# Scan outputs of a hybrid encoder layer: four chunks in one step for five of eight groups, with shared probability slots, a part of the decay subtraction on ScalarE and shorter warm-ups

## The chip, the cores and the metric

The kernel runs on one core of one Trainium2 chip. The metric is the device time of one execution in microseconds (us); lower is better. Three runs of the kernel before took 1091.04, 1091.76 and 1092.42 us, so the median is 1091.76 us.

## What is computed

One layer of a bidirectional encoder over 512 tokens of width 1024, in float32. After an RMSNorm, one input projection feeds two branches: a bidirectional chunked state-space scan (8 groups of 4 heads, chunks of 128 tokens) and a windowed attention (16 heads, 64 wide). Gates merge the branches, an output projection and a squared-ReLU MLP follow. The part that matters here is the output of the scan for one direction, for each chunk `l`, group `g` and head `r`:

```python
cb = jnp.einsum('bclgn,bcsgn->bcgls', c, b)
y_diag = jnp.einsum('bcgls,bcgrls,bcsgrp->bclgrp', cb, decay, xdt)
states = jnp.einsum('bclgn,bcgrl,bclgrp->bcgrpn', b, decay_states, xdt)
y_off = jnp.einsum('bclgn,bcgrpn,bcgrl->bclgrp', c, prev, jnp.exp(a_cs))
y = y_diag + y_off        # y_fwd + y_bwd + xs * d_skip, times silu(z), RMSNorm per group
```

In the attention, `p = exp(logits - m)` is divided by its sum before it is multiplied by the values.

## The kernel before, in words

**TensorE's work.** A matrix product in high precision is made of three products of `fp32r` operands: every weight and activation is split into a rounded part and the rest (`hi`, `lo`), and `mm3` issues hi·hi, hi·lo, lo·hi. A projection of 128 output columns over 512 tokens is 24 such matmuls into one PSUM bank of the pool `pp` (3 banks). Everything smaller goes to the pool `ps` (5 banks): transposes, attention scores, the scan's products. The scan's products and transposes are plain `f32`, and a plain `f32` matmul shows as two passes in the trace (a transpose as one).

**Half-width matmuls.** Two kinds of `ps` products write only 64 of 128 partitions, two heads side by side: `m,x` (the scan's diagonal part, `yd`, in `outs`) and `pT,V` (attention values, `attn_values`). In rows they read `128*64`. A stretch of such matmuls that follow each other is called a half-width run below. The other product of `outs` is `C,pv` (the states' part, `yo`, full width, one bank for each chunk).

**Weights.** Each weight chunk is loaded by SyncE's queue (`wr`), rounded by ScalarE (`wh<-wr`, L495) and the rest is made by GpSimd, at times VectorE (`wl<-wr,wh`, L499), three chunks ahead.

**The scan of a group** (`ssd_steps`): `load(c)` fetches rows of cumulative decays, broadcast to 128 partitions (`rf`, `rb`, and `E`); `prep(c)` (L1101 to L1126) makes the 128x128 weights `m` of four heads: GpSimd subtracts the columns `cs` from `rb` for all four heads at once (L1114), ScalarE adds `ncs` to `rf`, head by head (L1116), VectorE takes the minimum of the two (L1117), ScalarE the exponential, and so on; `outs(j)` (from L1128) makes the outputs of the chunks 1 and 0 (`j` = 0) or 2 and 3 (`j` = 1): 6 `C,pv` matmuls, 8 `m,x`, then VectorE's products with `E` (L1151) and the sum `w` (L1152), GpSimd's sums, ScalarE's square `sq` (L1162), GpSimd's `ssq` (L1164) and the split of `ssq` into `sh`, `sl` (L437, L438), which `rms` multiplies by ones on TensorE.

**The attention of a head**: `attn_scores` writes four probability tiles `P` (256, 384, 384 and 256 wide, each in a slot of its own), takes exponentials on ScalarE (L884) and multiplies by the reciprocal sums on VectorE (L890); `attn_flip` transposes them into `pT`; `attn_values` multiplies by `V`.

**The start**: `WARM` matmuls on a tile of zeros, the transpose of `g` (L610 copies it to `gT`), the load of `x`, its scale by ScalarE and VectorE (L640, L641), `DUMMY` matmuls on `x` of which the order puts one ahead of the eight transposes of `x` and the rest behind; VectorE and ScalarE then make `h` (L445, L446).

**What sets the order.** `Quantum`s of projection work give a program order, and `at` places the small steps between them (`SCAN`: `outs` at 2.5 and 5.5). Then a `Planner` with a cost for each instruction re-orders all of it, engine by engine, and `chain` fixes each engine's order. TensorE takes the first ready matmul in program order, but stays with a kind (`fp32r` or `f32`, full or half width) where it can (`next_matmul`), and takes a half-width matmul only when all that its bank waits for is done (`awaited`). Each engine runs its list strictly in that order, so a matmul whose input is late holds all that stand behind it.

Of the kernel before, what the change touches and what calls it, by code (L numbers as in the profile page):

```python
# [11 lines left out]
F32R = mybir.dt.float32r  # L12
AF = mybir.ActivationFunctionType
# [20 lines left out]
BACK = 3  # L34
WARM = 18
DUMMY = 6
COLD = 7000.0
# [41 lines left out]
class Slots:  # L79
# [13 lines left out]
    def put(self, *tiles):  # L93
        for t in tiles:
            self.free.append(self.slot.pop(id(t))[0])


class Planner:
# [13 lines left out]
    def __init__(self, instructions, tags):  # L112
        names = {"PE": "PE", "DVE": "DVE", "Activation": "ACT", "Pool": "POOL", "SP": "SP"}
        self.ins = [i for i in instructions if type(i).__name__ != "BassTilePoolBoundary"]
        self.eng = [names[str(i.engine).split(".")[-1]] for i in self.ins]
        self.tags = tags
        self.depend()
        self.cost = [self.duration(n) for n in range(len(self.ins))]
        self.kind = [self.matmul_kind(n) if e == "PE" else None for n, e in enumerate(self.eng)]
        self.awaited, banks = {}, {}  # L120
        for n, k in enumerate(self.kind):
            if k and k[1]:
                banks.setdefault(self.operands(self.ins[n].outs)[0].tensor.name, []).append(n)
        for bank in banks.values():
            needed = set().union(*(self.pre[n] for n in bank)) - set(bank)
            self.awaited.update((n, needed) for n in bank)

# [234 lines left out]
class Trunk:  # L362
# [498 lines left out]
    def attn_scores(self, h):  # L861
# [3 lines left out]
        mx, sm, es = (self.tmp(n, [128, 4], 4) for n in ("mx", "sm", "es"))  # L865
        P = []
        for n in range(4):
            j0, j1 = (128 if n == 0 else 0), (256 if n == 3 else 384)
            k0, w = n * 128 - 128 + j0, j1 - j0
            ps = self.bank("ps")  # L870
            tok = slice(n * 128, (n + 1) * 128)
            self.mm(ps[:, :w], q[:, tok], self.KH[j][:, k0:k0 + w], True, False)
            self.mm(ps[:, :w], q[:, tok], self.KL[j][:, k0:k0 + w], False, True)
            p = self.slots.get("P", (128, 384))
            nc.vector.tensor_tensor_reduce(p[:, :w], ps[:, :w], bt[:, j0:j1], 1.0, self.sink[:, h:h + 1],
                                           ALU.add, ALU.max, mx[:, n:n + 1])
            P.append((p, w))
# [10 lines left out]
        for n in range(4):  # L888
            p, w = P[n]
            nc.vector.tensor_scalar(p[:, :w], p[:, :w], sm[:, n:n + 1], None, op0=ALU.mult)  # L890
        self.P[h] = P

    def attn_flip(self, h):
        self.T[h] = []
        for n, (p, w) in enumerate(self.P.pop(h)):
# [3 lines left out]
            self.slots.put(p)  # L899
            pT = self.slots.get("pT", (128, 384))  # L900
            (self.nc.vector.tensor_copy if n % 2 else self.nc.scalar.copy)(pT[:, :w], pt[:, :w])
            self.T[h].append((pT, w))

    def attn_values(self, k):
# [12 lines left out]
        for pT, _ in T[0] + T[1]:  # L917
            self.slots.put(pT)
        hi, lo = self.slots.get("ah", dtype=F32R), self.slots.get("al", dtype=F32R)
# [112 lines left out]
    def ssd_steps(self, g):  # L1032
# [71 lines left out]
        def prep(c):  # L1104
            def run():
# [7 lines left out]
                m, n = get("m"), get("n")  # L1113
                nc.gpsimd.tensor_tensor(v4(rb), v4(rb), cs[:, 1].unsqueeze(2).to_broadcast([128, 4, 128]), op=ALU.subtract)  # L1114
                for h in range(4):
# [11 lines left out]

        def outs(j):  # L1128

            def run():  # L1130
                cs = (1, 0) if j == 0 else (2, 3)
                w = st["w"][j]
                yos = {}
                for c in cs:
                    yo = yos[c] = self.bank("ps").rearrange("p (d i t) -> p d i t", d=2, i=2)
                    for d in dirs[3 - c]:
                        for i in range(2):
                            S = st["enter"][c][:, d * 256 + i * 128:d * 256 + (i + 1) * 128]
                            self.mm(yo[:, d, i], S, st["C"][:, c * 128:(c + 1) * 128], True, True)
                yd = self.bank("ps").rearrange("p (c i t) -> p c i t", c=2, i=2)  # L1140
                for c in cs:
                    x, m = xs(c), ch[c]["m"]
                    for i in range(2):
                        for u in range(2):
                            h = 2 * i + u
                            self.mm(yd[u * 64:(u + 1) * 64, c % 2, i], x[:, h * 64:(h + 1) * 64], v4(m)[:, h], True, True)
                    put(m)
                for c in cs:
                    dd = slice(dirs[3 - c][0], dirs[3 - c][-1] + 1)
                    E = ch[c]["E"]  # L1150
                    nc.vector.tensor_tensor(E[:, dd], yos[c][:, dd], E[:, dd], op=ALU.mult)  # L1151
                nc.vector.tensor_tensor(w, yd, w, op=ALU.add)  # L1152
                for c in cs:
                    wc, E = w[:, c % 2], ch[c]["E"]
                    for d in dirs[3 - c]:
                        nc.gpsimd.tensor_tensor(wc, wc, E[:, d], op=ALU.add)  # L1156
                    nc.gpsimd.tensor_tensor(wc, wc, st["z"][j][:, c % 2], op=ALU.mult)
                    put(E)
                if "ssq" not in st:
                    st["ssq"] = get("ssq")  # L1160
                sq = get("sq", (128, 2, 2, 128))
                nc.scalar.activation(sq, w, AF.Square)  # L1162
                half = st["ssq"][:, j * 256:(j + 1) * 256].rearrange("p (c t) -> p c t", c=2)
                nc.gpsimd.tensor_tensor(half, sq[:, :, 0], sq[:, :, 1], op=ALU.add)  # L1164
                put(sq)
                if j == 1:
                    put(st["B"], st["C"], *st["bt"], *st["x"], *st["z"], *st["pv"])
                    hi, lo = st["sq"] = get("sh", dtype=F32R), get("sl", dtype=F32R)
                    self.split(hi, lo, st["ssq"])
                    put(st["ssq"])  # L1170
            return run

        def rms():
# [28 lines left out]

        return weigh, states0, states1, [load(c) for c in range(4)], [prep(c) for c in range(4)], [outs(j) for j in range(2)], rms, finish

# [9 lines left out]
    def place_ssd(self, g, q):  # L1214

        def place():
# [461 lines left out]
```

## Time and profile before

| | before |
|---|---|
| median of 3 runs | 1091.76 us (1091.04 to 1092.42) |
| the profiled execution's own time | 1091.93 us |
| its span, first to last instruction | 1090.1 us |
| TensorE (PE) busy | 1080.1 us (99%) |
| VectorE (DVE) busy | 740.1 us (68%) |
| ScalarE (ACT) busy | 642.9 us (59%) |
| GpSimd (POOL) busy | 794.5 us (73%) |
| mean granted TensorE clock | 0.997 of full speed |

The span lies 1.83 us under the execution's own time, which also holds what lies around the instructions. The profiled execution is 0.17 us above the median. "Busy" counts instructions from start to end as the profile models them; an engine can be busy all the time and still be held up between two of its instructions, so the distances between starts in the timeline are read beside it.

### The profile page before, as it was taken

Reading aid. Unit: us, or ns where it says so; the run is one execution under the profiler, and the core shown is the slowest. Engines: PE = TensorE matmul, PEld = TensorE weight load, DVE = VectorE, ACT = ScalarE, POOL = GpSimd, SP = SyncE. Lnnn points to the kernel's source line nnn. Section 1 sums busy time; section 2 is a strip of 40 time slices with the busy share of each in tenths; the row PEclk is TensorE's granted clock in tenths of the full one; section 3 lists DMA queues with packets and bytes.
Section 4 is the critical chain, followed back from the end, with each engine's and each line's share of the span. In section 5 each row is a group of like instructions: output and inputs, shape, how many; then the busy total and the mean of one; then the engine's idle time right before and its main releaser. Section 6 shows DMA issues by size and latency. Waiting matters only on the chain.

```text
span 1090.1 us, 16770 instructions
## 1 busy us (share of the span) xinstructions
PE 1080.1 (99%) x5631; PEld 906.1 (83%) x5631; DVE 740.1 (68%) x1288; ACT 642.9 (59%) x1379; POOL 794.5 (73%) x977
## 2 busy tenths in 40 slices
PE   9999999999999999999999999999999999999997
PEld 8888888888888888888888888889888888888885
DVE  5567788687788687778788753334672583583698
ACT  6566777686776777676769633323554544544552
POOL 3546657557668888988999876521588898898994
PEclk9999999999999999999999999999999999999998
DMA  7434433634354536354655554534322422424222
GB/s 205 127 95 129 117 94 95 157 90 118 100 123 127 145 101 174 97 141 134 162 138 140 145 173 121 165 103 155 92 70 71 153 74 83 154 74 147 90 97 77
DMA packets 209209, 132.31 MB, mean 121 GB/s; under 512 B 10538, under 2 KB 192042, under 8 KB 209123
## 3 DMA queue, kind: packets, MB, share of 16 engines
q1 hardware_dynamic: 208963, 131.18, 42.6%
q8 instruction: 44, 0.72, 0.3%
q14 instruction: 42, 0.34, 0.1%
q10 hardware_dynamic: 160, 0.07, 0.0%
HBM read 126.69 MB, written 4.52 MB: 120 GB/s over the span
## 4 chain that ended last, share of the span: by engine, by line
PE 98%; DVE 0%; DMA 0%; ACT 0%; issue 0%; POOL 0%; DVEq 0%; POOLq 0%; SPq 0%
PE pp L420 69%; PE ps L420 25%; PE ps L424 3%; DMA rb<-csT 0%; DVEq L1674 0%; DVE ag L1586 0%; DVE h L446 0%; POOLq L1674 0%; ACT h L445 0%; ACT wh L495 0%; SPq L1101 0%; PE pp L424 0%; POOL ssq L1164 0%; ACT x L640 0%; DVE acc L1564 0%
## 5 line engine op out<-in xcount | busy, mean ns | idle before, releaser
L499 POOL TENSOR_TENSOR wl<-wr,wh 128x256 fp32r<-128x256 f32 (+1 forms) x504 | 426.0, 873 | 153.5 <-ACT wh L495 141.7
L420 PE MATMUL pp<-h,wh 128*128 128x512 f32 (+1 forms) x1728 | 527.9, 388 | 0.0
L420 PEld LDWEIGHTS pp<-h,wh 128*128 128x128 f32 x1728 | 318.9, 188 | 64.1 <-issue 1.9
L420 PE MATMUL pp<-h,wl 128*128 128x512 f32 (+1 forms) x856 | 332.3, 388 | 0.0
L495 ACT CAST wh<-wr 128x1024 fp32r<-128x1024 f32 (+1 forms) x133 | 138.9, 1044 | 144.6 <-PE pp L420 125.2
L420 PEld LDWEIGHTS pp<-h,wl 128*128 128x128 f32 x856 | 160.9, 188 | 32.5 <-issue 0.5
L1512 POOL TENSOR_TENSOR wl<-wd,wh 128x256 fp32r<-128x256 f32 x158 | 131.1, 865 | 11.7 <-ACT wh L1509 11.6
L1509 ACT CAST wh<-wd 128x512 fp32r<-128x512 f32 x82 | 47.5, 621 | 32.8 <-PE ps L420 15.5
L420 PE MATMUL ps<-wl,fh 128*128 128x512 f32 x164 | 63.9, 390 | 0.0
L420 PE MATMUL ps<-wh,fl 128*128 128x512 f32 x164 | 63.8, 389 | 0.0
L420 PE MATMUL ps<-wh,fh 128*128 128x512 f32 x164 | 63.8, 389 | 0.0
L1379 DVE SCALAR_TENSOR_TENSOR pp<-pp,r 128x512 f32<-128x512 f32 (+1 forms) x31 | 17.6, 567 | 66.3 <-ACT r L1376 66.3
L1120 ACT ACTIVATE n<-cb,tables 128x128 f32<-128x128 f32 x128 | 49.5, 394 | 17.1 <-DVE cb L1111 16.6
L952 DVE SCALAR_TENSOR_TENSOR u<-pp,cv,u 128x510 f32<-128x510 f32 (+1 forms) x64 | 47.7, 745 | 4.5 <-ACT u L948 3.4
L420 PE MATMUL pp<-yh,wl 128*128 128x512 f32 x128 | 49.8, 390 | 0.0
L420 PE MATMUL pp<-yh,wh 128*128 128x512 f32 x128 | 49.7, 389 | 0.0
L420 PE MATMUL pp<-yl,wh 128*128 128x512 f32 x128 | 49.6, 389 | 0.0
L1121 ACT ACTIVATE m<-cb,tables 128x128 f32<-128x128 f32 x128 | 49.3, 393 | 0.3 <-DVE cb L1111 0.2
L1116 ACT ACTIVATE rf<-rf,tables 128x128 f32<-128x128 f32 x128 | 42.7, 396 | 11.2 <-DMA rf<-csT 11.1
L1156 POOL TENSOR_TENSOR w<-w,E 128x256 f32<-128x256 f32 x48 | 37.9, 803 | 13.1 <-DVE w L1152 11.8
L1050 POOL TENSOR_TENSOR xd<-x,tables 128x256 f32<-128x256 f32 x48 | 33.0, 705 | 17.8 <-ACT x L975 12.8
L884 ACT ACTIVATE P<-P,mx 128x384 f32<-128x384 f32 (+1 forms) x64 | 35.3, 554 | 15.6 <-DVE mx L881 15.3
(271 smaller groups left out, 2163.1 us busy)
## 6 DMA issues: line engine op xcount, KB each, us to landing
wr<-in_w_in SPq DMA_DIRECT2D x76, 512.0 KB, 4.0
wr<-in_w_mlp_in SPq DMA_DIRECT2D x32, 512.0 KB, 4.2
wd<-in_w_mlp_out SPq DMA_DIRECT2D x64, 256.0 KB, 6.3
rf<-csT SPq DMA_DIRECT2D x32, 256.0 KB, 4.8
rb<-csT SPq DMA_DIRECT2D x32, 256.0 KB, 3.7
wr<-in_w_ssd_out SPq DMA_DIRECT2D x14, 512.0 KB, 3.9
E<-csE SPq DMA_DIRECT2D x96, 64.0 KB, 4.2
x<-in_x SPq DMA_DIRECT2D x16, 256.0 KB, 4.2
```

Source lines behind the costliest of these rows:

```text
L420: self.nc.tensor.matmul(out, lhsT, rhs, start=start, stop=stop, skip_group_check=more)
L495: self.nc.scalar.copy(hi[:, :m], raw)
L499: engines[e].tensor_tensor(lo[:, c], raw[:, c], hi[:, c].bitcast(F32), op=ALU.subtract)
L884: nc.scalar.activation(p[:, :w], p[:, :w], AF.Exp, bias=mx[:, n:n + 1], accum_out=sm[:, n:n + 1])
L952: nc.vector.scalar_tensor_tensor(u[:, a:e], ps[:, a + d:e + d], self.wtap(t, b), u[:, a:e], op0=ALU.mult, op1=ALU.add)
L1050: nc.gpsimd.tensor_tensor(v4(xd[:, d * 256:(d + 1) * 256]), v4(xs(c)), by_dir(self.coef, c)[:, d].unsqueeze(2).to_broadcast([128, 4, 64]), ...
L1116: nc.scalar.activation(v4(rf)[:, h], v4(rf)[:, h], AF.Identity, bias=ncs[:, 0, h:h + 1])
L1120: nc.scalar.activation(v4(n)[:, h], cb[:, 0], AF.Copy, scale=dt[:, 0, h:h + 1])
L1121: nc.scalar.activation(v4(m)[:, h], cb[:, 1], AF.Copy, scale=dt[:, 1, h:h + 1])
L1156: nc.gpsimd.tensor_tensor(wc, wc, E[:, d], op=ALU.add)
L1509: nc.scalar.copy(hi, src)
L1512: (nc.vector if q == 512 else nc.gpsimd).tensor_tensor(lo[:, c], src[:, c], hi[:, c].bitcast(F32), op=ALU.subtract)
```

## The change

1. `outs` takes several `j`. For groups 0 to 4 (`JOINT`) one step at 5.5 (`BOTH`) makes all four chunks: the `C,pv` matmuls and `E` products of both halves, then the `m,x` matmuls of both halves (two `yd` banks), then the sums (`collect`). Groups 5 to 7 keep two steps at 2.5 and 5.5.
2. The planner's `awaited` set is made for a whole half-width run of the program order in place of one bank: no matmul of the run is taken before all inputs of the run are done.
3. `rb`: GpSimd subtracts for two of four heads; ScalarE does the other two.
4. The narrow tiles 0 and 3 of `P` and of `pT` share one slot; ScalarE scales these two in place of VectorE.
5. `WARM` goes from 18 to 14, `DUMMY` from 6 to 4.

```diff
+JOINT, BOTH = 5, 5.5
-WARM = 18
-DUMMY = 6
+WARM = 14
+DUMMY = 4
...
-        self.awaited, banks = {}, {}
+        self.awaited, runs, before = {}, [], None
         for n, k in enumerate(self.kind):
             if k and k[1]:
-                banks.setdefault(self.operands(self.ins[n].outs)[0].tensor.name, []).append(n)
-        for bank in banks.values():
-            needed = set().union(*(self.pre[n] for n in bank)) - set(bank)
-            self.awaited.update((n, needed) for n in bank)
+                if not before or not before[1]:
+                    runs.append([])
+                runs[-1].append(n)
+            before = k or before
+        for run in runs:
+            needed = set().union(*(self.pre[n] for n in run)) - set(run)
+            self.awaited.update((n, needed) for n in run)
...
-        P = []
+        P, edge = [], self.slots.get("P")
...
-            p = self.slots.get("P", (128, 384))
+            p = self.slots.get("P", (128, 384)) if 0 < n < 3 else edge[:, n // 3 * 256:n // 3 * 256 + 256]
...
-            nc.vector.tensor_scalar(p[:, :w], p[:, :w], sm[:, n:n + 1], None, op0=ALU.mult)
+            if 0 < n < 3:
+                nc.vector.tensor_scalar(p[:, :w], p[:, :w], sm[:, n:n + 1], None, op0=ALU.mult)
+            else:
+                nc.scalar.activation(p[:, :w], p[:, :w], AF.Copy, scale=sm[:, n:n + 1])
...
-                nc.gpsimd.tensor_tensor(v4(rb), v4(rb), cs[:, 1].unsqueeze(2).to_broadcast([128, 4, 128]), op=ALU.subtract)
+                nc.gpsimd.tensor_tensor(v4(rb)[:, 2:], v4(rb)[:, 2:], cs[:, 1, 2:].unsqueeze(2).to_broadcast([128, 2, 128]), op=ALU.subtract)
+                for h in range(2):
+                    nc.scalar.activation(v4(rb)[:, h], v4(rb)[:, h], AF.Identity, bias=ncs[:, 1, h:h + 1])
...
-        def outs(j):
+        def outs(*js):
             def run():
+                for j in js:
+                    yos = {}
+                    for c in ((1, 0), (2, 3))[j]:
...
+                        yos[c] = yo
+                    for c, yo in yos.items():
+                        dd = slice(dirs[3 - c][0], dirs[3 - c][-1] + 1)
+                        E = ch[c]["E"]
+                        nc.vector.tensor_tensor(E[:, dd], yo[:, dd], E[:, dd], op=ALU.mult)
+                for j in js:
+                    yd = st["yd", j] = self.bank("ps").rearrange("p (c i t) -> p c i t", c=2, i=2)
...
+                for j in js:
+                    collect(j)
...
-            for j in range(2):
-                self.at(q(o["outs"][j]), outs[j])
+            if g < JOINT:
+                self.at(q(BOTH), outs(0, 1))
+            else:
+                for j in range(2):
+                    self.at(q(o["outs"][j]), outs(j))
```

What the planner makes of it, at the two places that the prediction speaks of. TensorE, group 3, in the kernel before: the two half-width runs of the group stand apart, the first among projections (`pp`), the next one some 70 rows further on. Of the first:

```order
L420 MATMUL pp_4457<-h_108,wl_4263 128x512
L420 MATMUL ps_4478<-m_4299,x_3974 64x128 x4
L420 MATMUL ps_4478<-m_4401,x_3974 64x128 x4
L420 MATMUL ps_4529<-C_4082,B_3916 128x128
L420 MATMUL ps_4607<-C_4082,B_3916 128x128
```

And TensorE at the same group in the changed kernel, where the four chunks' `C,pv` and `m,x` stand together:

```order
L425 MATMUL ps_4658<-C_4069,pv_4268 128x128 x4
L425 MATMUL ps_4663<-C_4069,pv_4270 128x128 x2
L425 MATMUL ps_4668<-C_4069,pv_4269 128x128 x4
L425 MATMUL ps_4673<-C_4069,pv_4270 128x128 x2
L425 MATMUL ps_4678<-m_4285,x_3932 64x128 x4
L425 MATMUL ps_4678<-m_4389,x_3932 64x128 x4
L425 MATMUL ps_4687<-m_4494,x_3942 64x128 x4
L425 MATMUL ps_4687<-m_4574,x_3942 64x128 x4
L425 MATMUL pp_4645<-h_98,wh_4483 128x512
```

One half-width run of 16 matmuls (two banks) has taken the place of two of 8, right behind four `C,pv` banks. The same happens once in each of the groups 0 to 4; counted over the whole order, half-width runs go from 24 to 19.

VectorE at the start, before:

```order
L636 ISA junk_125,ssq_75<-x_121 128x512
L636 ISA ssq_75 128x1
L641 TENSOR_SCALAR x_121<-x_121,rst_76 128x512
L610 COPY gT<-ps_80 128x8
L499 TENSOR_TENSOR wl_167<-wr_162,wh_166 128x256 x2
```

And VectorE at the start of the changed kernel:

```order
L641 ISA junk_121,ssq_75<-x_117 128x512
L641 ISA ssq_75 128x1
L615 COPY gT<-ps_80 128x8
L646 TENSOR_SCALAR x_117<-x_117,rst_76 128x512
L504 TENSOR_TENSOR wl_161<-wr_156,wh_160 128x256 x2
```

The copy of `gT`, which waits for TensorE's transpose of `g` behind the warm-ups, now stands ahead of the scale of `x`, which TensorE's first matmul on `x` waits for.

## Rows read from the trace of the kernel before

**Rows 1.** By stretch: length; busy us of PE, PEld, DVE, ACT, POOL; granted clock; DMA.

```profile
60.00:345.00 285.00, 285.00 (x1730) 242.73 (x1729) 224.92 (x488) 206.03 (x500) 180.88 (x234) 1.00 0.42 111
345.00:606.00 261.00, 260.64 (x1400) 216.80 (x1399) 197.89 (x287) 187.22 (x424) 232.80 (x281) 1.00 0.53 140
```

**Rows 2.** The chain that ended last, by engine, from the page.

```profile
PE 98%; DVE 0%; DMA 0%; ACT 0%; issue 0%; POOL 0%; DVEq 0%; POOLq 0%; SPq 0%
```

**Rows 3.** Waits of TensorE after its first instruction (engine, tile, line, releaser: total us, times, longest).

```profile
PE ps L424 <- ACT x L640: 0.4, 1, 0.4
PE ps L420 <- ACT sh L437: 0.4, 1, 0.4
PE ps L420 <- ACT h L445: 0.3, 1, 0.3
```

**Rows 4.** Timeline of TensorE (start us, us, instructions): half-width runs and their neighbours.

```profile
131.70 2.40 PE L420 MATMUL ps<-pT,V 128*64 128x128 f32 x40
134.03 0.49 PE L420 MATMUL ps<-C,B 128*128 128x128 f32 x2
...
217.93 0.38 PE L420 MATMUL ps<-C,B 128*128 128x128 f32 x2
218.15 1.50 PE L420 MATMUL ps<-C,pv 128*128 128x128 f32 x12
...
222.94 0.39 PE L420 MATMUL pp<-h,wl 128*128 128x512 f32 x1
223.17 0.61 PE L420 MATMUL pp<-h,wh 128*128 128x512 f32 x2
223.71 1.09 PE L420 MATMUL ps<-m,x 128*64 128x128 f32 x16
224.74 0.49 PE L420 MATMUL ps<-C,B 128*128 128x128 f32 x2
225.06 0.38 PE L424 MATMUL ps<-ident,P 128*128 128x128 f32 x2
```

**Rows 5.** Timeline of the first 10 us, all engines.

```profile
1.03 6.64 PE L420 MATMUL ps<-zero 128*128 128x128 f32 x36 [1.03 <-DVE mhalf L599]
...
6.18 0.49 DVE L641 TENSOR_SCALAR x<-x,rst 128x512 f32<-128x512 f32 x1 [1.01 <-POOL rst L639]
...
7.60 0.22 PE L424 MATMUL ps<-ident,g 8*128 8x8 f32 x1
...
7.76 0.49 PE L420 MATMUL ps<-x 128*128 128x128 f32 x2
7.86 0.17 DVE L610 COPY gT<-ps 128x8 f32<-128x8 f32 x1 [1.19 <-PE ps L424]
...
9.05 0.63 ACT L445 ACTIVATE h<-pp,gT 128x128 fp32r<-128x128 f32 x2 [0.90 <-PE pp L424]
```

**Rows 6.** Timeline of TensorE cut at 2.0 to 5.9, 6.1 to 7.55, 6.1 to 7.2: warm-ups.

```profile
1.62 4.60 PE L420 MATMUL ps<-zero 128*128 128x128 f32 x21
...
5.89 1.78 PE L420 MATMUL ps<-zero 128*128 128x128 f32 x14
...
5.89 1.56 PE L420 MATMUL ps<-zero 128*128 128x128 f32 x12
```

**Rows 7.** Timeline of TensorE around its longest wait inside the scan.

```profile
572.75 0.40 PE L420 MATMUL pp<-h,wl 128*128 128x512 f32 x1
573.50 0.50 PE L420 MATMUL ps<-sh,ones_r 128*128 128x512 f32 x1 [0.36 <-ACT sh L437]
```

**Rows 8.** Groups by line and shape (count, busy us, mean ns of one, idle before).

```profile
L1114 POOL TENSOR_TENSOR rb<-rb,tables 128x512 f32<-128x512 f32 x32 | 34.8, 1089 | 7.3 <-DMA rb<-csT 7.2
...
L1116 ACT ACTIVATE rf<-rf,tables 128x128 f32<-128x128 f32 x128 | 42.7, 396 | 11.2 <-DMA rf<-csT 11.1
...
L890 DVE TENSOR_SCALAR P<-P,sm 128x256 f32<-128x256 f32 x32 | 14.6, 458 | 0.5
...
L1151 DVE TENSOR_TENSOR E<-ps,E 128x512 f32<-128x512 f32 x16 | 11.0, 685 | 5.2 <-PE ps L420 4.9
```

More of the change, by code (lines that the diff above doesn't have):

```diff
@@ L889, in attn_scores @@
             p, w = P[n]
-            nc.vector.tensor_scalar(p[:, :w], p[:, :w], sm[:, n:n + 1], None, op0=ALU.mult)
-        self.P[h] = P
+            if 0 < n < 3:
+                nc.vector.tensor_scalar(p[:, :w], p[:, :w], sm[:, n:n + 1], None, op0=ALU.mult)
+            else:
+                nc.scalar.activation(p[:, :w], p[:, :w], AF.Copy, scale=sm[:, n:n + 1])
+        self.P[h] = P, edge
     def attn_flip(self, h):
         self.T[h] = []
-        for n, (p, w) in enumerate(self.P.pop(h)):
+        P, old = self.P.pop(h)
+        edge = self.slots.get("pT")
+        for n, (p, w) in enumerate(P):
             pt = self.bank("ps")
@@ L898, in attn_flip @@
                 self.tr(pt[:, b * 128:(b + 1) * 128], p[:, b * 128:(b + 1) * 128])
-            self.slots.put(p)
-            pT = self.slots.get("pT", (128, 384))
+            pT = self.slots.get("pT", (128, 384)) if 0 < n < 3 else edge[:, n // 3 * 256:n // 3 * 256 + 256]
             (self.nc.vector.tensor_copy if n % 2 else self.nc.scalar.copy)(pT[:, :w], pt[:, :w])
             self.T[h].append((pT, w))
+        self.slots.put(old, P[1][0], P[2][0])
+        self.T[h].append((edge, 0))
     def attn_values(self, k):
@@ L916, in attn_values @@
                             b == 0, b == nb - 1)
-        for pT, _ in T[0] + T[1]:
-            self.slots.put(pT)
+        for t in T:
+            self.slots.put(t[1][0], t[2][0], t[4][0])
         hi, lo = self.slots.get("ah", dtype=F32R), self.slots.get("al", dtype=F32R)
@@ L1126, in prep @@
             return run
-        def outs(j):
+        def outs(*js):
             def run():
[L1131 to L1136, printed above, removed]
-                        for i in range(2):
[L1138 to L1170, printed above, removed]
-            return run
@@ new lines, in run @@
+                for j in js:
+                    yos = {}
+                    for c in ((1, 0), (2, 3))[j]:
+                        dd = slice(dirs[3 - c][0], dirs[3 - c][-1] + 1)
+                        yo = self.bank("ps").rearrange("p (d i t) -> p d i t", d=2, i=2)
+                        for d in dirs[3 - c]:
+                            for i in range(2):
+                                S = st["enter"][c][:, d * 256 + i * 128:d * 256 + (i + 1) * 128]
+                                self.mm(yo[:, d, i], S, st["C"][:, c * 128:(c + 1) * 128], True, True)
+                        yos[c] = yo
+                    for c, yo in yos.items():
+                        dd = slice(dirs[3 - c][0], dirs[3 - c][-1] + 1)
+                        E = ch[c]["E"]
+                        nc.vector.tensor_tensor(E[:, dd], yo[:, dd], E[:, dd], op=ALU.mult)
@@ new lines, in run @@
+                for j in js:
+                    yd = st["yd", j] = self.bank("ps").rearrange("p (c i t) -> p c i t", c=2, i=2)
+                    for c in ((1, 0), (2, 3))[j]:
+                        x, m = xs(c), ch[c]["m"]
+                        for i in range(2):
+                            for u in range(2):
+                                h = 2 * i + u
+                                self.mm(yd[u * 64:(u + 1) * 64, c % 2, i], x[:, h * 64:(h + 1) * 64], v4(m)[:, h], True, True)
+                        put(m)
@@ new lines, in run, with collect @@
+                for j in js:
+                    collect(j)
+            return run
+        def collect(j):
+            w = st["w"][j]
+            nc.vector.tensor_tensor(w, st.pop(("yd", j)), w, op=ALU.add)
+            for c in ((1, 0), (2, 3))[j]:
+                wc, E = w[:, c % 2], ch[c]["E"]
+                for d in dirs[3 - c]:
+                    nc.gpsimd.tensor_tensor(wc, wc, E[:, d], op=ALU.add)
+                nc.gpsimd.tensor_tensor(wc, wc, st["z"][j][:, c % 2], op=ALU.mult)
+                put(E)
+            if "ssq" not in st:
+                st["ssq"] = get("ssq")
+            sq = get("sq", (128, 2, 2, 128))
+            nc.scalar.activation(sq, w, AF.Square)
+            half = st["ssq"][:, j * 256:(j + 1) * 256].rearrange("p (c t) -> p c t", c=2)
+            nc.gpsimd.tensor_tensor(half, sq[:, :, 0], sq[:, :, 1], op=ALU.add)
+            put(sq)
+            if j == 1:
+                put(st["B"], st["C"], *st["bt"], *st["x"], *st["z"], *st["pv"])
+                hi, lo = st["sq"] = get("sh", dtype=F32R), get("sl", dtype=F32R)
+                self.split(hi, lo, st["ssq"])
+                put(st["ssq"])
@@ L1201, in finish @@
             self.grp[g] = None
-        return weigh, states0, states1, [load(c) for c in range(4)], [prep(c) for c in range(4)], [outs(j) for j in range(2)], rms, finish
+        return weigh, states0, states1, [load(c) for c in range(4)], [prep(c) for c in range(4)], outs, rms, finish
     def place_head(self, h, q):
```

## The prediction

> **What bounds the kernel now.** I read the stretches first, then the chain that ended last, then the waits of TensorE, then its timeline. In both stretches of the scan TensorE is busy for the whole length, 285.00 of 285.00 us and 260.64 of 261.00 us, at a granted clock of 1.00, which is the upper level of 2.4 GHz; ScalarE has about 72% in both (206.03 / 285 and 187.22 / 261), GpSimd 63% and 89% [rows 1]. The chain that ended last is TensorE for 98% [rows 2], and after its first instruction TensorE waits visibly three times, 0.4, 0.4 and 0.3 us [rows 3]. So a microsecond is won only if TensorE's own stream gets shorter, or one of its few waits goes; work taken from or given to another engine counts only where TensorE then waits more, or less.
>
> "Busy" hides one thing, which the distances of starts show. Two projection matmuls stand 0.23 us apart (222.94 to 223.17). The two that start at 223.17 should be over by 223.17 + 2 x 0.23 = 223.63, but the half-width run starts at 223.71: 0.08 us too late. Inside runs, 16 passes take 1.03 us to the next start (223.71 to 224.74) and 40 passes take 2.33 us (131.70 to 134.03), so one more pass costs (2.33 - 1.03) / 24 = 0.054 us and a run has 1.03 - 16 x 0.054 = 0.17 us that does not depend on its length. Behind the run the two `C,B` passes take 0.32 us (224.74 to 225.06) where they take 0.22 us with no such run ahead (217.93 to 218.15): 0.10 us more [rows 4]. A half-width run therefore costs 0.08 + 0.17 + 0.10 = 0.35 us beside its passes, whatever its length.
>
> **The change part by part.** The sum is made against the profiled execution's own time, 1091.93 us, which is 0.17 us above the median shown.
>
> *Joint steps.* All matmuls of the scan stay. The order has 24 half-width runs before and 19 after: in each of the groups 0 to 4 one run goes (in group 1, half of the first pair stood beside attention values already, and the joint run stands beside them now). 5 x 0.35 = 1.75 us off TensorE, all of it on the path, since TensorE is. The full-width `f32` stretches between them are joined too; I take nothing for that.
>
> *`awaited` for whole runs.* It moves only where runs stand and costs no instruction. Its price would be a run that is taken later, with projections in its place, which TensorE has anyway. Nothing.
>
> *The wait of 0.5 us in group 6.* TensorE's matmul on `sh` starts at 573.50, when the one before it started at 572.75 and needs 0.23: 0.52 us lost, to ScalarE's `sh` [rows 7]. In the changed order the second `m,x` run of that group stands 14 projection matmuls earlier (14 x 0.23 = 3.2 us), and VectorE's part of `sl` stands ahead of a `cb` and two `rf` in place of behind them. What feeds `sh` should then come earlier by more than 0.52. I take the wait as gone; at worst it stays (0).
>
> *`rb` on ScalarE.* GpSimd loses half of 32 operations of 1.089 us, and ScalarE gains 64 operations of 0.396 us, which overlap to 42.7 / 128 = 0.334 us each: 21.4 us over the scan [rows 8]. This is beside TensorE: ScalarE goes from 72% by 21.4 us in 546 to about 76%. If that cover were gone, the weights `m` of a chunk would come up to 2 x 0.334 = 0.67 us later.
>
> *Probability tiles.* VectorE loses 32 scalings of 0.458 us [rows 8] and ScalarE gains them. A ScalarE operation on 256 columns lies between 0.396 (128 columns, the row above) and twice that, so at most 32 x 0.79 = 25 us in the first stretch, which brings it to at most (206 + 25 + 12) / 285 = 85%. Hidden, and the sharing of a slot removes no transfer.
>
> *The start.* The warm-ups begin at 1.03, in 36 passes. The third to the 23rd start from 1.62 to 5.89, (5.89 - 1.62) / 20 = 0.21 us apart; behind that, 14 passes end at 7.67 and 12 of them at 7.45, so two take 0.22, 0.11 us each [rows 6]. The clock column reads 1.00 all along, but these distances say that the passes run at the lower level, 1.2 GHz, up to about 6 us and at 2.4 GHz behind it. The four removed matmuls are 8 passes. The rise comes during the passes that are kept, so what goes is 8 x 0.11 = 0.89 us. The transpose of `g` moves from 7.60 to 6.71. But VectorE's order has changed: before, it scaled `x` at 6.18, long ahead of need; now it copies `gT` first. That copy follows the transpose by 0.26 (7.60 to 7.86) and takes 0.17, so it ends at 6.71 + 0.43 = 7.14, `x` is scaled by 7.14 + 0.49 = 7.63, and TensorE's first matmul on `x`, at 7.76 before [rows 5], can start near 7.66. Most of the 0.89 turns into a wait of TensorE for VectorE. The transposes behind it feed `h` (ScalarE, 9.05, which waited 0.90 us for them), and from there TensorE follows ScalarE and VectorE. I take 0.10, with 0 and 0.89 as ends. The two dummy matmuls less (4 passes) end TensorE's queue earlier at 10 us, where it waits for `h` anyway: nothing.
>
> A rule speaks against trimming here. In the rows the rise comes with the warm-ups still running, and what goes lies behind it. The Trainium skill (TensorE: Matmul & The Clock Gate, part 1) says that the engine starts at half clock until work releases it, and that the moment of the release varies from run to run. By the rows the trim costs nothing in clock and the sum stands; by the rule a run with a late release would be about 1.0 us longer, the rival below.
>
> *New waits.* The kernel before has one wait of 0.52 us inside the scan. That is what this planner left in 546 us, so another order of its making may have none or one such: I take 0.3 us, with ends of 0 and 1.5 (three like the one in rows 7).
>
> *Sum.* 1091.93 - 1.75 - 0.52 - 0.10 + 0.3 = 1089.9 us for an execution like the profiled one; 0.17 less for the median: **1089.7 us**, 2.0 us or 0.19% under the median shown. With the ends of the unknown terms: lowest 1091.76 - 1.75 - 0.52 - 0.89 = 1088.6, highest 1091.76 - 1.75 + 1.5 = 1091.5.
>
> **The rivals.**
>
> *ScalarE becomes late (gain given back).* ScalarE gets 21 to 47 us more, and its list is strictly in order, so the copy that frees a PSUM bank, or the rounding of a weight chunk, now stands behind subtractions that wait for the load of `rb` (GpSimd waited 7.2 us for it in all [rows 8]). For: ScalarE at up to 85%. Against: weights are split three chunks ahead, and TensorE never waits for one in rows 3. If one wait like that of rows 7 came in four of the eight groups, 4 x 0.52 = 2.1 us, the time would be 1091.8: no change.
>
> *Slower: the second `yd` bank is late.* In the groups 1 to 4 the order puts the half-width run straight behind `C,pv`. The pool `ps` has five banks, and the joint step wants four for `yo` and two for `yd`, so the sixth comes only when an `E` product of VectorE, 0.685 us [rows 8], has freed the first, and all projections stand behind the run. If TensorE had to wait there for all four products, two of 0.685 and two on half the columns, 2.06 us less the 0.87 us of the first bank's 16 passes, that is 1.2 us in each of five groups, 6.0 us: 1089.7 + 6.0 = 1095.7. It decides from 4.2 us on, 0.85 a group. Against: the first product can start while three more banks of `C,pv` run, and the planner takes no run before it holds the inputs for done.
>
> *Late clock.* If the rise came only behind the 28 kept passes, the matmuls on `x` and the transposes ahead of `h`, some 10 passes, would take 0.21 in place of 0.11 us each: 1.0 us later, 1090.7. Against: in rows 6 the rise came at pass 23 or soon behind it, five passes ahead of the end of what is kept. The Trainium skill's rule above points to this case.
>
> *The start gives all it has.* If VectorE's swap does not bind, 0.8 more is won: 1088.9.
>
> *The runs' cost is not all saved.* If the 0.17 us inside a run belonged to its bank and not to the run, a joint run would pay it twice: 5 x 0.17 = 0.85 less is won, 1090.5. Against: a joint run stays in one mode from its first pass to its last.
>
> **How the numbers follow.** The forecast as it stands, with the waits of a new order between 0 and 1 us: 0.72. The start gives all: 0.06. Late ScalarE: 0.09. Late clock: 0.04. Runs' cost not saved: 0.05. Second bank late, slower: 0.04. A measurement of this kernel tells about 0.2%, 2.2 us, from no change, so the lines are 1089.6 and 1093.9. The forecast lies 0.1 us from the first: of its 0.72 I put 0.36 on each side. Faster: 0.36 + 0.06 = 0.42. Slower: 0.04. Within: the rest, 0.54. The range, 1088.6 to 1091.4, holds the forecast with its ends, the full start, the late clock and the unsaved runs, and leaves out the slower case, the late ScalarE and the tails.
>
> **What would show it.** Right: 19 half-width runs, each with the same fixed 0.35 us; five of them with 32 passes of `m,x`; TensorE's first matmul on `x` near 7.7, with a wait for VectorE ahead of it; no wait for `sh` in group 6; ScalarE busy some 35 us more, and TensorE's chain still 98%. Wrong: a row of waits of TensorE for `E`, `m` or `x` at the joint runs; a fixed cost that grows with the run; transposes of `x` at 7.2 us.

## The result, and the profile after

The changed kernel is slower: 1096.97 us median of six runs (1093.44 to 1098.04) against 1092.11 before, ratio 1.0041, 95% interval 1.0027 to 1.0056. The forecast was 1089.7 us, with 1088.6 to 1091.4 as its range. The profiled execution took 1097.02 us, its span is 1095.2 us.

Line numbers of the changed kernel are 5 to 21 higher than those of before in the parts spoken of here. The same two stretches as [rows 1], changed kernel:

```profile
60.00:345.00 285.00, 279.74 (x1700) 238.43 (x1699) 206.85 (x447) 217.43 (x541) 155.89 (x215) 0.99 0.42 111
345.00:606.00 261.00, 260.96 (x1395) 218.47 (x1394) 201.68 (x297) 202.75 (x474) 232.82 (x295) 1.00 0.52 138
```

TensorE was idle for 5.26 us of the first stretch, where the mean granted clock is 0.99, and for next to nothing of the second. ScalarE is at 76% and 78%, within what was reckoned. The chain that ended last, which was TensorE for 98% [rows 2], and the waits of TensorE, to be laid beside [rows 3]:

```profile
PE 95%; DVE 2%; ACT 2%; DMA 1%; issue 1%; POOL 0%; DVEq 0%; POOLq 0%; SPq 0%
```

```profile
PE ps L425 <- ACT pT L910: 3.1, 2, 2.7
PE ps L425 <- DVE pT L910: 1.8, 1, 1.8
...
PE ps L425 <- DVE x L646: 0.7, 1, 0.7
PE ps L429 <- ACT x L645: 0.4, 1, 0.4
PE ps L429 <- ACT P L898: 0.3, 1, 0.3
```

The wait for `sh` is gone. New are waits of attention scores for copies of transposed probability tiles (`pT`), which have to free a PSUM bank, and a short one for a probability tile `P` that ScalarE scales. Timeline of TensorE where they stand:

```profile
189.82 0.39 PE L425 MATMUL pp<-h,wl 128*128 128x512 f32 x1
190.54 1.31 PE L429 MATMUL ps<-ident,P 128*128 128x128 f32 x10 [0.33 <-ACT P L898]
...
191.81 0.28 PE L425 MATMUL ps<-KL,Q 128*128 128x256 f32 x1
194.76 0.44 PE L425 MATMUL ps<-KH,Q 128*128 128x384 f32 x1 [2.67 <-ACT pT L910]
195.03 0.34 PE L425 MATMUL ps<-KL,Q 128*128 128x384 f32 x1
197.17 0.69 PE L425 MATMUL ps<-KH,Q 128*128 128x384 f32 x1 [1.80 <-DVE pT L910]
197.66 0.52 PE L425 MATMUL ps<-KL,Q 128*128 128x384 f32 x1
...
200.53 0.63 PE L425 MATMUL pp<-h,wh 128*128 128x512 f32 x2
```

Behind the waits the matmuls are slow as well; by stretch (columns as in [rows 1]):

```profile
194.00:197.00 3.00, 0.62 (x2) 0.30 (x2) 3.00 (x4) 2.34 (x5) 2.94 (x3) 1.00 0.14 39
197.00:200.50 3.50, 3.33 (x9) 2.89 (x10) 3.15 (x13) 1.31 (x4) 2.93 (x5) 0.51 0.82 222
```

For 3.5 us the granted clock was 0.51, the lower level of 1.2 GHz, after 3 us in which TensorE had worked 0.62.

Why are the copies late? ScalarE's timeline says that it sat idle for 6.39 us until VectorE had negated the row maxima `mx`, and from there worked its list down in order, with the copy near the end:

```profile
186.61 0.62 ACT L889 ACTIVATE P<-P,mx 128x384 f32<-128x384 f32 x1 [6.39 <-DVE mx L886]
...
194.35 0.73 ACT L910 COPY pT<-ps 128x256 f32<-128x256 f32 x2
```

And VectorE's and GpSimd's timelines say where the 6.4 us are:

```profile
179.96 6.62 DVE L886 TENSOR_SCALAR mx<-mx 128x4 f32<-128x4 f32 x1
186.49 1.52 DVE L963 SCALAR_TENSOR_TENSOR C<-pp,cv,C 128x510 f32<-128x510 f32 x2
```

```profile
179.46 1.44 POOL L1185 TENSOR_TENSOR ssq<-sq 128x256 f32<-128x256 f32 x2
180.87 2.82 POOL L504 TENSOR_TENSOR wl<-wr,wh 128x256 fp32r<-128x256 f32 x4
183.64 2.33 POOL L1061 TENSOR_TENSOR xd<-x,tables 128x256 f32<-128x256 f32 x4
185.93 0.61 POOL L1125 TENSOR_TENSOR rb<-rb,tables 128x256 f32<-128x256 f32 x1
```

One multiplication by -1, of four elements in each partition, took 6.62 us. All 16 of its kind (least, median and longest ns):

```profile
L886 DVE TENSOR_SCALAR mx<-mx x16: 158/171/6615, 58.1 to 335.1; 128x4 f32<-128x4 f32 x16
```

It began while GpSimd was in the first of eleven instructions that ran without a gap, and ended at 186.58 with the last of them, at 186.54. I call that *shut out* from here on, and such a row of GpSimd instructions a *train*. Of the time: by start distances the waits are 0.49 us (190.54 - 189.82, less a projection's 0.23), 2.83 us (194.76 - 191.81, less the 0.12 that such a matmul takes), 1.97 us (197.17 - 195.03, less 0.17), and two smaller ones for copies at 234.55 and 235.22, 0.80 together. These last two are not shown to come from the shut-out. The chain behind them leads to ScalarE, whose list had waited for the load of `rf`:

```profile
221.69 1.28 ACT L1129 ACTIVATE rf<-rf,tables 128x128 f32<-128x128 f32 x4 [2.37 <-DMA rf<-csT]
```

### The profile page after: what moved, and what is told of

Same layout as the page of the kernel before. It is cut to its first block, busy times and chain, and to the rows that moved or that the text cites. A ratio compares the mean times of both kernels' runs of the same rounds, so it can differ in the third digit from the quotient of the medians.

```text
span 1095.2 us, 16820 instructions
## 1 busy us (share of the span) xinstructions
PE 1079.3 (99%) x5619; PEld 906.7 (83%) x5619; DVE 725.3 (66%) x1256; ACT 671.4 (61%) x1475; POOL 771.7 (70%) x977
## 4 chain that ended last, share of the span: by engine, by line
PE 95%; DVE 2%; ACT 2%; DMA 1%; issue 1%; POOL 0%; DVEq 0%; POOLq 0%; SPq 0%
PE pp L425 67%; PE ps L425 24%; PE ps L429 3%; DMA rf<-csT 1%; DVE mx L886 1%; ACT wh L500 0%; ACT P L889 0%; DVE xl L1066 0%; ACT n L1133 0%; DVE yT L1215 0%; ACT m L1134 0%; DVE P L880 0%; ACT P L898 0%; DVEq L1697 0%; DVE ag L1609 0%
## 5 line engine op out<-in xcount | busy, mean ns | idle before, releaser
L504 POOL TENSOR_TENSOR wl<-wr,wh 128x256 fp32r<-128x256 f32 (+1 forms) x504 | 419.5, 862 | 180.3 <-ACT wh L500 178.0
```

The lines of the kernel that those rows point to most:

```text
L504: engines[e].tensor_tensor(lo[:, c], raw[:, c], hi[:, c].bitcast(F32), op=ALU.subtract)
```

## The experiments

Theory A: VectorE was shut out by GpSimd, and that is the loss. Theory B: ScalarE has too much to do. Theory C: the joint step itself crowds the PSUM banks. First, is it a chance of one execution?

### e1: the changed kernel again

No edit.

> The changed kernel as it is, timed again and profiled a second time. Theory A (port): in the first profile one VectorE instruction of four elements, the negation of the row maxima at 179.96 us, took 6.62 us instead of 0.17 and ended with the last of eleven GpSimd instructions that ran without a gap; four copies of probability tiles behind it in VectorE's order and on ScalarE came late, and TensorE waited 2.83 + 1.96 us for their PSUM banks and then ran at a granted clock of 0.5 from 197.09 to 200.50 us. If the order of the instructions brings this about, the long negation stands in this profile too, within 1 us of the same place, and the median is 1096 to 1098 us. Theory M (a chance of one execution): the negation takes under 0.7 us here and the time is 1090 to 1092. Theory B (ScalarE has too much to do): about 1097, with or without the long negation.

Measured: 1096.96 us median of 12 runs, ratio 1.0042 (1.0028 to 1.0057), but from 1090.01 to 1101.67: eight runs at 1096.92 or above, four at 1094.22, 1092.44, 1091.85 and 1090.01. The profiled execution is the one of 1090.01, 0.3 us from the forecast. The same instructions in it, VectorE's and TensorE's timelines:

```profile
179.46 0.28 DVE L886 TENSOR_SCALAR mx<-mx 128x4 f32<-128x4 f32 x1
180.47 3.10 DVE L963 SCALAR_TENSOR_TENSOR C<-pp,cv,C 128x510 f32<-128x510 f32 x4 [0.73 <-ACT C L959]
183.50 0.47 DVE L891 TENSOR_TENSOR sm<-sm,es 128x4 f32<-128x4 f32 x1
```

```profile
190.77 0.28 PE L425 MATMUL ps<-KL,Q 128*128 128x256 f32 x1
190.89 0.34 PE L425 MATMUL ps<-KH,Q 128*128 128x384 f32 x1
191.06 0.34 PE L425 MATMUL ps<-KL,Q 128*128 128x384 f32 x1
192.12 0.44 PE L425 MATMUL ps<-KH,Q 128*128 128x384 f32 x1 [0.72 <-DVE pT L910]
192.40 0.33 PE L425 MATMUL ps<-KL,Q 128*128 128x384 f32 x1
...
193.95 0.62 PE L425 MATMUL pp<-h,wh 128*128 128x512 f32 x2
```

Here the negation took 0.28 us, one wait of 0.72 us is left at this place, and the clock stays up. From 192.40 to 193.95 stand the matmuls that took from 197.66 to 200.53 in the execution of 1097.02 us: 2.87 us against 1.55, so the low clock cost 1.3 us, and 0.2 more in the matmul ahead (0.49 against 0.28 us to the next start). Two executions of one program, 7.0 us apart. Laid side by side matmul for matmul, the one of 1097.02 loses 0.5 us before 12 us, 0.5 at 190.54, 5.6 from there to 200.53 and 0.8 at 234 to 235, and gets 0.4 back later. The negation is the largest difference between them and not the first: e1 was half a microsecond ahead from the start, because its warm-ups came to the upper clock level earlier (4.73 us for the same 28 passes in place of 5.72):

```profile
1.03 4.73 PE L425 MATMUL ps<-zero 128*128 128x128 f32 x28 [1.03 <-DVE mhalf L604]
...
7.06 0.49 PE L425 MATMUL ps<-x 128*128 128x128 f32 x2 [1.14 <-DVE x L646]
```

Theory M is half right: the shut-out is a matter of the execution, but by the times it comes in most of them; of the eight runs at 1096.92 or above none was profiled. What the runs between 1091.85 and 1094.22 met was not profiled either. That this execution lies so near the forecast is in part luck: its start gave 0.7 us in place of 0.1, and its waits for copies took 1.5 us (0.89 at 192.12, 0.62 at 303.30) where 0.3 was put for new waits.

### e2 and e3: the negation in another form

```diff
-        nc.vector.tensor_scalar(mx, mx, -1.0, None, op0=ALU.mult)
+        nc.vector.tensor_reduce(mx, mx.unsqueeze(2), AX.X, ALU.max, negate=True)
```

The planner's cost for it is held, so the order is that of the changed kernel (e2) and of the kernel before (e3), row for row.

> The changed kernel with the 16 negations of the row maxima done by a reduction over one element with negation instead of a multiplication by -1; the order of every engine's instructions is the same, row for row. Theory A: the reduction is not shut out by GpSimd, so the 5.1 us of waits (2.83 + 1.96 + 0.31) and the stretch at half clock (197.09 to 200.50 us, of which 2.87 us of matmul distances would have been 1.49, so 1.4 us) go: 1097.0 - 6.5 = 1090.5 us (1089.5 to 1091.5). Theory B (ScalarE's added subtractions and scalings make the copies of transposed probabilities late): nothing changes, 1096 to 1098 us. The Trainium skill, SBUF - State Buffer, Per-engine ports, names the reduction as a form that never contends with GpSimd for the shared pair and the scalar multiplication as one that can.

> The kernel before with the same exchange and the same order. Its longest negation took 0.57 us, so by theory A there is nothing to win: 1091.5 to 1092.5 us, ratio 0.999 to 1.001. If the exchange by itself makes a kernel faster for another reason (the reduction is shorter, fewer port conflicts elsewhere), it is below 1091 here too, and e2 proves less.

e2: 1092.39 us (1090.92 to 1095.41), ratio 1.0006 (0.9997 to 1.0014): 4.6 us less than e1, not the 6.5 expected. e3: 1092.31, ratio 1.0004 (0.9996 to 1.0013): the exchange by itself brings nothing. In e2's profile the negation takes 0.156 us, but VectorE's timeline has a new victim, the addition of row sums and sink terms, and its end falls again on the end of GpSimd's train:

```profile
182.72 3.30 DVE L891 TENSOR_TENSOR sm<-sm,es 128x4 f32<-128x4 f32 x1
```

```profile
183.10 2.32 POOL L1061 TENSOR_TENSOR xd<-x,tables 128x256 f32<-128x256 f32 x4
185.39 0.61 POOL L1125 TENSOR_TENSOR rb<-rb,tables 128x256 f32<-128x256 f32 x1
```

Theory B falls: ScalarE has the same work in the same order here. The order is the same row for row, so what took 4.6 us off the median is the form of the one instruction. Theory A stands with a correction: it is not this instruction alone, but another one of this chain can meet the train.

### e4: no joint steps, with e2's negation

```diff
-JOINT, BOTH = 5, 5.5
+JOINT, BOTH = 0, 5.5
```

> e2 with no joint step: the scan outputs of every group in two steps of two chunks again, the rest of the change kept. The planner then orders 24 runs of half-width matmuls instead of 19. By theory A and the sum of the prediction (0.35 us for each run) it is slower than e2 by 5 x 0.35 = 1.75 us, so about 1092.2 us (1091.2 to 1093.2). Theory C (it is the joint step that crowds the PSUM banks and makes TensorE wait): e2 stays at 1096 to 1098 and this one falls to about 1092. If the run saves nothing, it equals e2.

1091.82 us, ratio 1.0000 (0.9991 to 1.0008), no wait for `pT`, none shut out. Neither theory gets its number: e2 is 0.6 us slower than this, where A had it 1.75 faster and C some 5 slower. With instructions of e2 still shut out, the pair does not tell them apart.

### e5: GpSimd and VectorE alone

> A program that does nothing of the layer: 64 trains of eleven GpSimd subtractions (128x256, both operands in SBUF) without a gap, and in each train one small VectorE instruction (the probe) that comes at a moment which shifts by 31 ns from train to train: 16 times the multiplication of 4 elements by -1, 16 times a minimum of two SBUF tensors of 4 elements, 16 times the reduction with negation, 16 times a minimum of 256 elements with a scalar column. Theory A: probes of the first, second and fourth kind wait at least for the GpSimd instruction under way (up to 0.7 us) and some of them for several or for all that is left of the train (up to 6 us); the reduction always takes under 0.25 us. Rival: a VectorE instruction always gets in at the next boundary, no probe takes over 1.2 us, and the 6.62 us in the changed kernel and the 3.30 us of e2's addition come from something else.

The four probes (line, form, count: least, median and longest ns):

```profile
L39 DVE TENSOR_SCALAR w<-w x16: 170/534/736, 7.3 to 136.5; 128x4 f32<-128x4 f32 x16
...
L42 DVE TENSOR_TENSOR w<-w,es x16: 164/495/731, 144.7 to 274.2; 128x4 f32<-128x4 f32 x16
...
L45 DVE TENSOR_REDUCE w<-w x16: 156/157/159, 282.3 to 411.8; 128x4 f32<-128x4 f32 x16
...
L48 DVE TENSOR_SCALAR w<-w,es x16: 353/688/922, 419.9 to 550.3; 128x256 f32<-128x256 f32 x16
```

Half of theory A is shown, half not. Scalar operations and two-tensor operations wait for the end of the GpSimd instruction under way, the reduction never does. But no probe waited for a second one. The Trainium skill (SBUF — State Buffer, Who interferes with whom; the heading that e2's expectation gives is not on that page) has this rule: VectorE's scalar operations on SBUF, where their operands allow a mode that uses both ports, and its operations on two SBUF tensors share ports with a GpSimd instruction that reads SBUF, the one that starts first holds them for its whole instruction, and on this chip reductions stay out of it. The probes agree, up to 0.736 us for four elements. What the rule does not say is that ten further instructions can pass, as they did at 179.96.

### e6 and e7: the sum in another form too

```diff
-        nc.vector.tensor_tensor(sm, sm, es, op=ALU.add)
+        nc.vector.tensor_reduce(sm, se, AX.X, ALU.add)
```

`se` holds row sums and sink terms side by side. Order as in the changed kernel; e7 has `JOINT = 0` besides.

> e2 with the addition behind it exchanged too: row sums and sink terms lie side by side and a reduction over two elements adds them (in e2's profile that addition of 4 elements took 3.30 us, and TensorE then waited 1.97 us at 193.54). The order of all engines stays. Theory A: with both small instructions out of GpSimd's reach the long waits go; the profile of e1, in which no instruction was shut out, had a time of 1090.0 with 0.88 + 0.63 us of waits left, so the median is 1090.0 us (1089 to 1091) and the scatter of the runs falls from 11.7 us (e1) and 4.5 us (e2) to under 3 us. Theory C (the joint step crowds the banks): 1092 or more, as e2.

> e6 with no joint step (24 runs of half-width matmuls instead of 19). By the sum of the prediction slower than e6 by 5 x 0.35 = 1.75 us: about 1091.8 us (1091 to 1092.5), as e4. If the runs of half-width matmuls are worth nothing, it equals e6.

e6: 1090.56 us, eleven runs within 2.2 us (1089.58 to 1091.77), ratio 0.9988 (0.9979 to 0.9996): faster than before, 6.4 us less than e1 with the same order. Theory C is out as the main cause. The profile is of the slowest run, and there the next in the chain was shut out, the first of two scalings of probability tiles:

```profile
183.08 0.15 DVE L891 TENSOR_REDUCE es<-sm 128x4 f32<-128x8 f32 x1
183.26 0.18 DVE L892 RECIPROCAL es<-es 128x4 f32<-128x4 f32 x1
...
183.47 3.12 DVE L896 TENSOR_SCALAR P<-P,es 128x384 f32<-128x384 f32 x1
```

Three profiles, three victims, one train of GpSimd. A shut-out need not cost much: behind this one, at 192.63, TensorE waited 0.79 us for a copy, where e1 with none shut out had 0.72. (Another wait of 0.97 us stands at 304.41, far from it.) e7: 1091.52 us, 0.96 slower than e6, not 1.75; the two intervals overlap. The sign is right. In the profiles, which are of e6's slowest run and of e7's fastest, e6 has 1.8 us of waits for copies and e7 none.

### e8, e10, e11: later transposes

```diff
-HEADS = dict(scores=0, flip=2, values=3.5)
+HEADS = dict(scores=0, flip=2.5, values=3.5)
```

e8 is e6 with this, e10 the changed kernel with this alone, e11 the kernel before.

> e6 with the transposes of the probability tiles (the flips) half a place later behind the scores, so that the chain negation, exponential, sum, reciprocal, scaling has some 3 us more. Theory A: the waits for copies of transposed tiles that are left in e1 (0.88 us at 192.12, 0.63 at 303.30) go too, and a delay of one GpSimd instruction costs nothing: 1088.5 us (1087.5 to 1090). If a new order brings new waits: 1090 to 1093.

> The changed kernel with the flips half a place later (as e8) and the two small instructions as the change has them, a multiplication and an addition of two tensors. Tells what of e8's 1089.24 us is the slack and what the reductions. Theory A: with the new order a VectorE instruction can still be shut out (not seen in before, seen in three of four profiles of the change's order), but has some 3 us more before TensorE waits: 1089 to 1091 us, single runs above 1092. If the reductions are what counts: 1095 or more. If the slack is all: 1089.2, the same as e8.

> The kernel before with the flips half a place later. Control for e8 and e10: before has no wait for a transposed tile of over 0.15 us to win back, and the planner orders 25 runs of half-width matmuls instead of 24 (+0.35): 1092.1 us (1091.3 to 1093). If it falls below 1090.5, e8's gain over before is the flips' and not the change's.

e8: 1089.24 us (1087.93 to 1089.99), ratio 0.9972 (0.9962 to 0.9983), the fastest of all. e10: 1089.74 (1088.78 to 1092.45), ratio 0.9983 (0.9974 to 0.9992): the later transposes do nearly all, without the reductions. Whether by their slack is not shown: e10's profile has no instruction shut out, so the new order may just as well meet no train. e11: 1094.26, ratio 1.0025 (1.0016 to 1.0034), above the 1093 that was the most expected: before gets slower by the same edit, so the later transposes alone bring no gain; it takes the rest of the change with them. TensorE's waits in e8; none is for `pT`:

```profile
PE ps L425 <- DVE m L1136: 1.1, 1, 1.1
...
PE ps L425 <- DVE h L451: 0.4, 1, 0.4
```

### e12: the parts moved to ScalarE, moved back

e8 with `rb` for four heads on GpSimd and all four scalings on VectorE (the change's lines at 1125 to 1127 and 895 to 898 undone).

> e8 with two parts of the change undone: the subtraction for all four heads on GpSimd, the scaling of all four probability tiles on VectorE; joint steps and shared slots stay, 19 runs of half-width matmuls. By the prediction both parts are hidden and cost and bring nothing: 1089.2 us (1088.5 to 1090). If ScalarE was what held the chain back, it is faster than e8; if GpSimd's longer trains and VectorE's more two-port instructions bring shut-outs, slower, 1091 or more.

1089.80 us, ratio 0.9985 (0.9976 to 0.9994), beside e8's 0.9972 (0.9962 to 0.9983): the same within their intervals. Its profiled execution was the slowest of eleven, 1093.25, with two instructions shut out:

```profile
182.14 5.49 DVE L443 TENSOR_TENSOR sl<-ssq,sh 128x512 fp32r<-128x512 f32 x1
...
258.43 4.21 DVE L895 TENSOR_SCALAR P<-P,es 128x256 f32<-128x256 f32 x1
```

From 182 to 300 us TensorE waits 1.4 us in all here, in four short waits. Behind the 6.62 us in the first profile it was 4.8 (0.33 + 2.67 + 1.80). That speaks for the slack, but the orders differ, so it is no proof.

### e9 and e13: the train rebuilt

As e5, with the changed kernel's train of eleven; e13 adds ScalarE copies and 512 KB transfers.

> As e5, which showed no probe that waited past the GpSimd instruction under way (longest 0.74 us for 4 elements): 192 trains with the very sequence of the changed kernel at 179.5 to 186.5 us (two sums of halves, four differences written as fp32r, four products with a broadcast table, one subtraction with a broadcast table), and the probe (96 times the multiplication of 4 elements, 96 times the two-tensor minimum) at moments between 0.5 and 5 us into the train. Theory A1 (this sequence shuts VectorE out by its own make-up): some probes take over 1.5 us and end with the train. Theory A2 (it needs more than the two engines: ScalarE's or the DMA's part in the full kernel): none takes over 1.2 us.

> e9 with ScalarE copying 128x512 tiles from the start of each train on and with transfers of 512 KB each running through the first half of the program. Theory A3 (ScalarE's or the transfers' traffic makes the shut-out): some of the 96 probes of the first kind take over 1.5 us. Otherwise the longest stays under 1.2 us as in e9 (0.77), and the ingredient stays open.

The longest of 192 probes took 0.774 us in e9 and 0.778 in e13. Neither the make-up of the train (A1) nor this traffic (A3) brought a shut-out by itself in 192 probes each, and what lets GpSimd keep the ports stays open.

### e14: the worth of the joint step, once more

e8 with `JOINT = 0`.

> e8 with no joint step (24 runs of half-width matmuls instead of 19). By the sum of the prediction 5 x 0.35 = 1.75 us slower than e8: 1091.0 us (1090.3 to 1091.7). By what e7 against e6 showed, 0.96 us: 1090.2. If the joint step costs in waits what it saves in runs, the same as e8: 1089.2.

1093.51 us, ratio 1.0018 (1.0009 to 1.0027): 4.3 us slower than e8, where the sum had 1.75 and e7 had 0.96. Half-width runs are 24 against 19, each with 0.27 to 0.39 us beside its passes where no wait stands in it (0.22 in one of only 4 passes), so about 1.75 of it would be the sum's; the rest is the new order's. With JOINT the planner reorders all engines, and a pair of orders differs by more than the part under test. In this profile a VectorE instruction of the last stage took 5.96 us at 1034.45, and TensorE has no wait there.

## Why the prediction was wrong

By its own steps, against the profile of 1097.02 us:

- *Joint steps, 1.75 us.* Right. 19 half-width runs, each with 0.31 to 0.39 us beside its passes, whether 16, 32, 40 or 72 of them, but for one of 4 passes with 0.22. Added up, that is 8.5 us over the 24 runs of before and 6.6 over these 19. A joint run of 32 passes, TensorE's timeline:

```profile
393.36 1.97 PE L425 MATMUL ps<-m,x 128*64 128x128 f32 x32
395.26 0.74 PE L425 MATMUL pp<-h,wh 128*128 128x512 f32 x2
```

  1.90 us to the next start, less 32 x 0.054, is the same 0.17 as for 16 passes [rows 4]: the rival of costs not saved is out.
- *The wait for `sh`, 0.52.* Right: 578.88 to 579.12, where 0.23 is a projection's own time.

```profile
578.88 0.40 PE L425 MATMUL pp<-h,wl 128*128 128x512 f32 x1
579.12 0.40 PE L425 MATMUL ps<-sh,ones_r 128*128 128x512 f32 x1
```

- *The start, 0.10.* Right in kind, 0.18 in size: the matmul on `x` starts at 7.58 and waits for VectorE, where 7.76 stood before [rows 5]. Neither a late clock nor the whole 0.89, in these two executions, whose warm-ups come to the upper clock level at 6.1 and 5.9 us. Elsewhere that moment decides more than the trim: by the spacing of the warm-ups it lies between 3.9 us (e1) and 7.0 (e11) in the thirteen profiles of full kernels, and the first matmul on `x` between 7.02 (e2) and 7.89 (e14) with the new start, between 7.50 (e3) and 8.22 (e11) with the old one. The rule that the prediction sets against the trim, that the moment differs from run to run, is borne out.

```profile
6.69 0.22 PE L429 MATMUL ps<-ident,g 8*128 8x8 f32 x1
7.58 0.49 PE L425 MATMUL ps<-x 128*128 128x128 f32 x2 [0.67 <-DVE x L646]
```

- *`rb` and probability tiles, nothing.* Right as far as e12 can tell.
- *ScalarE becomes late.* The waits look like that rival, 3.1 us of them are for ScalarE's copies. But ahead of the long ones ScalarE had been idle for 6.39 us, and e6, with the same work in the same order for it, is 6.4 us faster at the median. It may hold for the 0.80 us at 234 to 235, where ScalarE's list had waited 2.37 us for a load; in e1 that wait was 0.80 us and TensorE had none at this place. ScalarE was busy 28.5 us more over the whole span (642.9 to 671.4), not some 35.
- *The second `yd` bank late.* No: in the profile after, TensorE waits for no `E` and no `m`.
- *New waits, 0.3 with ends of 0 and 1.5.* **This step failed.** They are 0.49 + 2.83 + 1.97 + 0.80 = 6.1 us, and 1.5 us of low clock behind them: 7.6. With that the sum reads 1091.93 - 1.75 - 0.52 - 0.18 + 7.6 = 1097.1, against 1097.02 measured. I had bounded the step by the waits that the old order has, as if a planner that leaves 0.5 us once leaves 0.5 us always. But its order is right only while each instruction takes the time that it reckons with. Its costs know the collision with the one GpSimd instruction under way (`port` in `plan`), not with a whole train: a VectorE operation that takes 0.28 us in one execution and 6.62 in another is not in them, nor was it in mine.

Was there a sign of it in the trace of before? The longest of the 16 negations there took 0.57 us, and most of those that met GpSimd took 0.26 to 0.57: proof that the two collide, but for one instruction at a time. The 35 runs of before beside e1 to e4 lie within 2.4 us. The collisions could have been read, the length of the worst could not.

The change does what it was reckoned to do: in the order as it is, an execution without a shut-out took 1090.01, and with two small operations out of reach 1090.56 is the median. (The range's upper end, by the way, should have been 1091.5 by the prediction's own sum, not 1091.4; it makes no difference here.) What made the changed kernel slower is shown as far as this: VectorE's operations stood still for 3 to 7 us, in forms that share ports with GpSimd, until a GpSimd train ended (the first profile, e2, e6), and the loss went when two of them had other forms in the same order (e6). It went as well with the transposes half a place later (e10), by slack or by another order. Not shown is why a shut-out comes. That the joint step or the moved parts bring it about is not shown either: the profiles of before, e3, e4, e7 and e11, all with two steps, have none, but e14 has one, in another stage, and e1, e8 and e10, with joint steps, have none.

## What to carry to other kernels

When a change makes a planner write a new order, the parts can be reckoned one by one, but the order's own waits belong in the range at the size of the longest delay that one instruction can suffer, not of the waits that are left over now. Look for a short VectorE instruction that ScalarE or TensorE waits for and that stands beside a long gapless row of GpSimd work: give it a form that takes no shared port, as the reductions of e6, or try what half a place of slack behind it brings. Time such a kernel more than six times, and read two profiles of the same program before explaining one.

## What the runs showed of the hardware

- A VectorE instruction can be kept waiting for several GpSimd instructions in a row: it took 6.62 us, 3.30, 3.12, 5.49, 4.21 and 5.96 us in six cases in thirteen profiles of full kernels. None of the 432 scalar and two-tensor operations in e5, e9 and e13, set beside such trains on purpose, waited for more than the one under way.
- A reduction on the same four elements took 0.156 to 0.159 us in all 16 probes of e5, with GpSimd at work beside it.
- TensorE's granted clock fell to 0.51 for 3.5 us after 2.67 and 1.80 us of waiting with 0.62 us of work between 194 and 197, and cost 1.5 us. In e1, with a single wait of 0.72 us at the same place, it stayed at 1.00.
- At the start of a program the moment of the clock's rise differs from execution to execution: 3.9 us in e1, 5.9 in the first profile, of the same kernel.
